# Two RMS norms applied as factors after the products, activations kept in freed buffers, and four PSUM banks per product

## The chip, the cores and the metric

The kernel runs on one core of one Trainium2 chip. The metric is device time in microseconds (us) of one execution. The engines are TensorE (PE: matmuls, with its weight loads listed apart as PEld), VectorE (DVE), ScalarE (ACT), GpSimd (POOL, which issues the gathers of table rows here) and SyncE (SP, which issues the other DMAs). Matmul results go to PSUM, of which this kernel uses all eight banks of 128 x 512 floats; all else lives in SBUF.

## The reference

One layer of a hybrid decoder is computed for 512 prompt tokens and 64 sample tokens together (576 columns), with D = 1024:

```
xn = rmsnorm(x) * attn_norm_g;  z = xn @ w_in          # q k v su sv gate_a gate_b: 30 blocks of 128 columns
a  = window attention(q, k, v);  m = gelu(su) * spatial_gate(LN(gelu(sv)))
x1 = x + (sigmoid(g_a) * (a @ w_branch_a) + sigmoid(g_b) * (m @ w_branch_b)) @ w_out
t  = rmsnorm(x1) * ffn_norm_g
s  = (t @ w_q) . sub_keys                              # 8 heads, two halves, 128 keys each
best 16 of the sums of the two halves' top 16;  gate = softmax(best)
x2 = x1 + sum_k gate_k * gelu(t . U[idx_k]) * V[idx_k] # 16384 experts
x3 = x2 + sigmoid(rmsnorm(x2) @ w_ple_gate) * (p @ w_ple)
```

A norm's factor 1/rms is one positive number per token. So it can be applied to a product's result as well as to its input, and the top 16 of a token's scores are the same with or without it; only the softmax of them needs it.

## The kernel before, in words

The work is tiled by 128. Every weight and every left operand is split in two fp32r parts, `hi` and `lo` (`split`: an ACT copy, then a DVE subtraction), and a product is three matmuls per 128 of depth (`tform`): 24 matmuls for a full product. `joint` makes a product for the 576 tokens in two halves of 256 and 320 columns, each in one PSUM bank from `mm()`, a pool of two banks, and hands each to an eviction. `load_block` loads a weight block of 512 KB (four buffers) and splits it (three buffers for each part), at high priority.

The stages, in the order in which TensorE comes to them:

1. `normed(xT, ...)`: squares of the eight pieces of x (`sumsq`, ACT), summed (DVE); ten small matmuls with ones give a column of sums, `rs` is 1/rms, a diagonal of it times ones gives the factor as a row in PSUM. Then each piece is multiplied (DVE, L164) and split: 16 pieces of half the columns.
2. The 30 blocks of `w_in` (`w_chunk`), evicted by ACT (copy, gelu or sigmoid). Attention and the spatial gate run beside them, one step after each block.
3. `w_br`: eight blocks, in each the two branches, evicted by DVE (L475).
4. `w_out`: eight blocks; x1 = result + x, again squares and sums. The per-layer embedding product `ple` fills in behind.
5. `normed(x1, ...)`, the second norm: as in 1, and it keeps copies of two groups of tokens, which `make_xr` turns by 16 transposes into rows for the gathers.
6. `peer_wq`: 16 query blocks (`joint`), each followed by the scores against 128 keys (`key_scores`), of which DVE finds the top 16 for each of five token tiles.
7. The experts. 128 prompt and 64 sample tokens use gathered rows (POOL fetches a row of U or V per token and choice; DVE multiplies and sums). The other 384 tokens go through all experts: `stage1(j)` is a product of 24 matmuls of 384 columns with the j-th block of U and a gelu; `build_g(tb)` makes the gates of 16 tokens as one-hot matrices on ACT and DVE and multiplies them on TensorE, and writes them to DRAM (`gd`); `stage2` multiplies activations by gates and adds the product with the j-th block of V to six PSUM banks.
8. The last norm and gate, and the output.

Stage 7 has an order of its own. `retrieve` (DVE, some ACT) is the choice of the 16 experts of a token tile, in steps; `stage1` calls stand between its steps. 62 calls of `stage1` come before the first `stage2`: the first NSP go out to DRAM (`ad`) and are read back later; 35 stay in a ring of RING buffers. In the last loop, over j, the first NSP + 1 turns have `stage2` alone, the next 66 have a `stage1` and a `stage2` each, and the rest `stage2` alone. `pay` sets how many gathered rows are fetched per turn.

A scheduler sets the order of the instructions on each engine from the order of the code and from priorities. Each engine takes its instructions strictly in that order, so an instruction that waits holds up all behind it on its engine.

Of the kernel before, what the change touches and what calls it, by code (L numbers as in the profile page):

```python
# [17 lines left out]
P = 128  # L18
D = 1024
# [9 lines left out]
NSP = 27  # L29
NAS = 12  # L30
# [7 lines left out]
RING = 36  # L38
# [8 lines left out]
def tile_decoder_step(ctx: ExitStack, tc: tile.TileContext, a, o):  # L47
# [74 lines left out]
    def tt():  # L122
        return e1.tile([P, NT], F32, name="t", bufs=4)
# [22 lines left out]
    def normed(x, tot, bk, gcol, hi, lo, keep=None):  # L146
        ps = bk()
        for c0, r in TILES:
            T.matmul(ps[:r, c0 // P:c0 // P + 1], lhsT=tot[:, c0:c0 + r], rhs=ones[:, 0:1], start=True, stop=True)
        rs = e1.tile([P, 5], F32, name="rs", bufs=1)  # L150
        for r, c in ((P, slice(0, 4)), (NS, slice(4, 5))):
            A.activation(rs[:r, c], ps[:r, c], AF.Sqrt, scale=1.0 / D, bias=eps[:r, 0:1])
            V.reciprocal(rs[:r, c], rs[:r, c])
        for cols in HALVES:
# [7 lines left out]
            for k in range(KC):  # L162
                xn = tt()[:, cols]
                V.scalar_tensor_tensor(xn, x[k][:, cols], vecs[:, gcol + k:gcol + k + 1], rstd,  # L164
                                       op0=ALU.mult, op1=ALU.mult)
                split(xn, hi[k][:, cols], lo[k][:, cols])
                if keep is not None:
                    keep(k, xn, cols)
# [16 lines left out]
    w_chunk(0, lambda ps, cols: A.activation(kraw[:, cols], ps, AF.Copy))  # L185
    bo = cload("blockones", [P, P])
# [259 lines left out]
    for i in range(24):  # L446
        if i < 8:
            t, g = (svT, suT)[i // 4], i % 4
            w_chunk(6 + i, lambda ps, cols: A.activation(t[:, g, cols], ps, AF.Gelu_apprx_tanh))
        else:  # L450
# [20 lines left out]
    for c in range(KC):  # L471
        w = load_block(a["w_br"][c])
        for i, (x, k0_) in enumerate(((ahl, 0), (mhl, 4))):
            sg = sgs[2 * c + i]
            joint(w, x, lambda ps, cols: V.tensor_tensor(sg[:, cols], sg[:, cols], ps, op=ALU.mult), k0_, 4)  # L475
# [40 lines left out]
    xk, xd = row((P, KC, P)), row((P, KC, 2, NS))

    def keep(k, xn_, cols):
        if cols.start == 0:
            A.activation(xk[:, k, :], xn_[:, 0:P], AF.Copy)  # L520
        else:
            A.activation(xd[:, k], xn_[:, 512 - cols.start:][:, None, :].to_broadcast([P, 2, NS]), AF.Copy)

    xn2_4 = [[x4(), x4()] for _ in range(2)]
    xn2 = [[q[k // 4][:, k % 4, :] for k in range(KC)] for q in xn2_4]
# [6 lines left out]
    tk = pool(tks, "tk", 2, "right")

    def make_xr():
        for src in (xd.rearrange("p k u t -> p k (u t)"), xk):
            xr_t = gp.tile([P, D], F32, name="xr")
            for hh in range(2):
                pt = bank("pt")
                for k in range(4):
                    T.transpose(out=pt[:, k * P:(k + 1) * P], in_=src[:, hh * 4 + k, :], identity=ident)  # L540
                A.activation(xr_t[:, hh * 512:(hh + 1) * 512], pt, AF.Copy)
            xrs.append(xr_t)
# [543 lines left out]
```

## Time and profile before

| | us |
|---|---|
| three runs | 1824.76, 1827.74, 1828.55 |
| median | 1827.74 |
| the profiled execution | 1827.41 |
| its span in the trace | 1825.7 |
| TensorE busy | 1771.8 (97%) |
| VectorE busy | 1417.3 (78%) |
| ScalarE busy | 871.0 (48%) |
| GpSimd busy | 531.6 (29%) |

The profile is of one execution. Lines such as L81 are lines of the kernel's file; nearly all products have L81, since a helper records them, so the tile names tell them apart: `x` is the split input, `c` a tile of a pool of large ones, `mm`, `sc`, `pt` and `pv` are PSUM banks, `oacc` the six accumulators of stage 2. A row of the view of waits reads "who <- whom: us in total, times, longest us". A row of a view by stretches gives, for each engine, busy us and the number of instructions, then TensorE's granted clock as a share of full speed, the share of time in which the DMA engines were busy, and GB/s.

### The profile page before, as it was taken

What the parts mean: (1) busy time and instruction counts of PE and PEld (TensorE: products, weight loads), DVE (VectorE), ACT (ScalarE), POOL (GpSimd) and SP (SyncE); (2) the same over time, 40 slices, a digit from 0 to 9 for tenths busy, and PEclk for the clock granted to TensorE, in tenths of its full rate; (3) what the DMA queues carried; (4) which work ended last, traced back from release to release, by engine and by line L of the source; (5) the groups of instructions that cost most, each with busy time, mean ns of one, the idle gap of its engine ahead of it and who ended that gap; (6) DMA issues with size and microseconds to landing.
All of it is one profiled execution on the core that took longest, in us unless ns stands there. A gap on an engine that the chain in (4) does not pass through costs nothing.

```text
span 1825.7 us, 27790 instructions
## 1 busy us (share of the span) xinstructions
PE 1771.8 (97%) x10094; PEld 1599.7 (88%) x10094; DVE 1417.3 (78%) x2846; ACT 871.0 (48%) x1560; POOL 531.6 (29%) x390
## 2 busy tenths in 40 slices
PE   6999999999998999999998999999999999999998
PEld 5987998989998999999976799989989899987776
DVE  6245446547889999999778898888888888899963
ACT  5476434244235688999732333333333333333441
POOL 0000000000002111455124565544444545466500
PEclk9999999999999999999999999999999999999999
DMA  7211223351226686999999999999999999999842
GB/s 222 86 47 47 70 79 125 115 165 64 74 72 207 217 249 221 342 355 348 336 333 346 355 410 393 356 372 331 357 378 325 361 370 327 326 348 376 325 133 75
DMA packets 177465, 458.18 MB, mean 251 GB/s; under 512 B 15664, under 2 KB 77872, under 8 KB 175280
## 3 DMA queue, kind: packets, MB, share of 16 engines
q1 hardware_dynamic: 121744, 254.34, 40.1%
q0 software_dynamic: 55584, 202.07, 30.2%
q8 instruction: 79, 1.29, 0.3%
q14 instruction: 58, 0.48, 0.1%
HBM read 419.72 MB, written 37.36 MB: 250 GB/s over the span
## 4 chain that ended last, share of the span: by engine, by line
PE 55%; DVE 3%; DMA 3%; issue 3%; POOL 1%; ACT 1%; DVEq 0%; POOLq 0%; ACTq 0%
PE mm L81 25%; PE oacc L907 23%; PE sc L792 2%; DMA x1c<-ad 2%; PE oacc L867 2%; PE pv L792 1%; PE pt L792 1%; POOL row L679 1%; DVE acc L698 1%; PE mm L867 1%; DVE w_lo L66 1%; DMA gs<-gd 1%; DMA row<-peer_v,idx 0%; DVE wl L66 0%; ACT w_hi L65 0%
## 5 line engine op out<-in xcount | busy, mean ns | idle before, releaser
L81 PE MATMUL mm<-x,w_hi 128*128 128x384 f32 (+2 forms) x3776 | 911.0, 326 | 14.7 <-ACT aS L745 8.9
L81 PEld LDWEIGHTS mm<-x,w_hi 128*128 128x128 f32 x3776 | 655.9, 191 | 36.4 <-ACT aS L745 11.1
L81 PE MATMUL mm<-x,w_lo 128*128 128x384 f32 (+2 forms) x1888 | 609.4, 323 | 0.0
L65 ACT ACTIVATE w_hi<-w_raw 128x1024 fp32r<-128x1024 f32 x325 | 344.0, 1059 | 452.7 <-PE mm L81 356.0
L66 DVE TENSOR_TENSOR w_lo<-w_raw,w_hi 128x1024 fp32r<-128x1024 f32 x325 | 396.5, 1221 | 150.8 <-ACT w_hi L65 145.9
L679 POOL DMA_INDIRECT row<-peer_u,idx x192 | 254.0, 1323 | 890.7 <-DVE pos L600 537.2
L81 PEld LDWEIGHTS mm<-x,w_lo 128*128 128x128 f32 x1888 | 359.0, 190 | 3.4 <-issue 3.2
L679 POOL DMA_INDIRECT row<-peer_v,idx x192 | 276.1, 1438 | 268.4 <-DVE acc L698 233.4
L907 PE MATMUL oacc<-w_hi,wl 128*128 128x512 f32 x768 | 244.1, 400 | 7.0 <-DVE wl L66 7.0
L907 PE MATMUL oacc<-w_hi,wh 128*128 128x512 f32 x768 | 244.9, 399 | 5.8 <-ACT wh L65 5.8
L698 DVE SCALAR_TENSOR_TENSOR acc<-row,wts,acc 128x1024 f32<-128x1024 f32 x192 | 245.2, 1277 | 2.3 <-DMA row<-peer_v,idx 2.0
L907 PE MATMUL oacc<-w_lo,wh 128*128 128x512 f32 x768 | 243.5, 398 | 0.0
L691 DVE SCALAR_TENSOR_TENSOR row<-row,xr 128x1024 f32<-128x1024 f32 x192 | 231.0, 1217 | 3.3 <-DMA row<-peer_u,idx 3.2
L907 PEld LDWEIGHTS oacc<-w_hi,wl 128*128 128x128 f32 x768 | 145.1, 190 | 44.8 <-DVE wl L66 10.4
L907 PEld LDWEIGHTS oacc<-w_lo,wh 128*128 128x128 f32 x768 | 145.7, 190 | 35.5
L907 PEld LDWEIGHTS oacc<-w_hi,wh 128*128 128x128 f32 x768 | 144.0, 189 | 37.3 <-ACT wh L65 7.7
L65 ACT ACTIVATE wh<-aL 128x384 fp32r<-128x384 f32 x65 | 34.1, 525 | 160.3 <-PE oacc L907 154.5
L781 ACT ACTIVATE oa<-oa,ew 128x128 f32<-128x128 f32 x192 | 86.0, 488 | 0.3
L780 ACT ACTIVATE oa<-c_iota,ew 128x128 f32<-128x128 f32 x192 | 67.2, 397 | 0.0
L792 PE MATMUL sc<-ob,oa 128*128 128x128 f32 x384 | 60.1, 279 | 1.4 <-DVE ob L783 1.3
L65 ACT ACTIVATE wh<-aS 128x384 fp32r<-128x384 f32 x36 | 18.9, 525 | 88.8 <-PE oacc L907 88.8
L66 DVE TENSOR_TENSOR wl<-aL,wh 128x384 fp32r<-128x384 f32 x65 | 36.6, 564 | 29.7 <-ACT wh L65 29.1
(293 smaller groups left out, 1721.3 us busy)
## 6 DMA issues: line engine op xcount, KB each, us to landing
w_raw<-peer_uT SPq DMA_DIRECT2D x128, 512.0 KB, 6.5
w_raw<-peer_v SPq DMA_DIRECT2D x128, 512.0 KB, 6.5
gd<-gs SPq DMA_DIRECT2D x24, 1024.0 KB, 9.1
gs<-gd SPq DMA_DIRECT2D x16, 1536.0 KB, 10.2
w_raw<-w_in SPq DMA_DIRECT2D x30, 512.0 KB, 3.3
w_raw<-peer_wq SPq DMA_DIRECT2D x16, 512.0 KB, 3.4
ad<-aS SPq DMA_DIRECT2D x27, 192.0 KB, 4.3
x1c<-ad SPq DMA_DIRECT2D x27, 192.0 KB, 5.5
```

The source lines that it names most:

```text
L65: A.activation(hi, src, AF.Copy)
L66: V.tensor_sub(lo, src, hi.bitcast(F32))
L81: mark_pe[0] = T.matmul(ps, lhsT=w[wi][:, wk + k, :], rhs=x[xi][k], start=i == 0, stop=i == n - 1)
L679: ins = G.indirect_dma_start(out=row_, out_offset=None, in_=table, in_offset=bass.IndirectOffsetOnAxis(ap=ix, axis=0))
L691: V.scalar_tensor_tensor(row_, row_, 1.0, xrs[ti], op0=ALU.mult, op1=ALU.mult, accum_out=dots[:, s:s + 1])
L698: V.scalar_tensor_tensor(accs[ti], row_, wts[:, s:s + 1], accs[ti], op0=ALU.mult, op1=ALU.add)
L780: A.activation(oa[:, t, :], iota, AF.Abs, bias=ew[:, 0, c + t:c + t + 1])
L781: A.activation(oa[:, t, :], oa[:, t, :], AF.Relu, scale=ew[:, 4, c + t:c + t + 1], bias=ew[:, 2, c + t:c + t + 1])
L792: T.matmul(pt[:, t * P:(t + 1) * P], lhsT=oa[:, t, :], rhs=ob[:, t, :], start=True, stop=True)
L867: T.matmul(ps[hh][:r], lhsT=xi[:, k, :r], rhs=w[k][wi][:, hh * 512:(hh + 1) * 512], start=k == 0 and xi is xh and wi == 0, stop=k == KC - ...
L907: mark_pe[0] = T.matmul(oacc[t][hh], lhsT=wi[:, ts], rhs=vi[:, hh * 512:(hh + 1) * 512], start=j == 0 and last == 0 and vi is vh, stop=j = ...
```

## The change

- The first norm: x times `attn_norm_g`, without 1/rms, is split and goes into the `w_in` products. 1/rms is copied to SBUF as a row `rn`, and every eviction of a `w_in` product becomes a DVE multiplication by `rn`; gelu, sigmoid and the query's square then run on ACT in place. The squares, their sums and `rn` have a raised priority. The first weight block is loaded between the second and third piece of x.
- The second norm: x1 times `ffn_norm_g` is split in the `w_out` loop (`xg`) and goes into the 16 query products. The factor enters the softmax as the scale of its exponential. The rows for the gathers come straight from the transposes of x1 (eight more small matmuls double the sample tokens), multiplied by factor and gain (DVE). The normed input of `stage1` is made later, in query blocks 3 to 10 (`norm_x`), from x1 in DRAM.
- `w_br`: the second branch's halves go to the two `sc` banks. `stage1`: every other product goes to the two `pv` banks until the last loop, and `build_g` uses `sc` and `pt` alone.
- Buffers: 24 of the ring's activations and six for those on their way to DRAM lie in tiles of the pool `x4`, which is free by then. RING goes from 36 to 44 and NSP from 27 to 19, so still 62 calls of `stage1` come first.

```diff
-NSP = 27
-NAS = 12
+NSP = 19
-RING = 36
+RING = 44
+NXP = 24
...
-def joint(w, x, out, wk=0, nk=KC):
+def joint(w, x, out, wk=0, nk=KC, bk=mm):
...
-    add(k, xT[k])
-normed(xT, tot, lambda: bank("sc"), 0, *xn)
+    with tc.high_priority(offset=500):
+        add(k, xT[k])
+    A.activation(xn[0][k], xT[k], AF.Copy, scale=vecs[:, k:k + 1])
+    V.scalar_tensor_tensor(xn[1][k], xT[k], vecs[:, k:k + 1], xn[0][k].bitcast(F32),
+                           op0=ALU.mult, op1=ALU.subtract)
+rn = e1.tile([P, NT], F32, name="rn", bufs=1)
+with tc.high_priority(offset=500):
+    for cols, ps in rstd_rows(tot, lambda: bank("sc")):
+        A.activation(rn[:, cols], ps, AF.Copy)
...
-def w_chunk(c, out):
-    joint(load_block(a["w_in"][c]), xn, out)
+def w_chunk(c, dst, out):
+    def scaled(ps, cols):
+        with tc.high_priority(offset=1000):
+            V.tensor_tensor(dst[:, cols], ps, rn[:, cols], op=ALU.mult)
+        out(cols)
+    joint(load_block(a["w_in"][c]) if c else first, xn, scaled)
...
     joint(w, x, lambda ps, cols: V.tensor_tensor(sg[:, cols], sg[:, cols], ps, op=ALU.mult), k0_, 4,
+          (mm, lambda: bank("sc"))[i])
...
+    A.activation(xg[0][c], x1[c], AF.Copy, scale=gcol)
+    V.scalar_tensor_tensor(xg[1][c], x1[c], gcol, xg[0][c].bitcast(F32), op0=ALU.mult, op1=ALU.subtract)
...
-normed(x1, tot, lambda: bank("sc"), 8, *xn2, keep=keep)
+rstd_cols(tot, rs2)
+def norm_x(k):
+    xc = tq.tile([P, NB], F32, name="xc")
+    S.dma_start(xc, x1d[k])
+    V.scalar_tensor_tensor(xc, xc, vecs[:, 8 + k:9 + k], rn2, op0=ALU.mult, op1=ALU.mult)
+    split(xc, xn2[0][:, k, :], xn2[1][:, k, :])
...
-A.activation(gt, gt, AF.Exp)
+A.activation(gt, gt, AF.Exp, scale=rs2[:, b_:b_ + 1])
...
-ps = mm()[:, :NB]
+ps = (mm() if j % 2 or phase[0] > 1 else bank("pv"))[:, :NB]
```

Three places show how the order of instructions moves. The first is DVE at the start of the program. Before (`rstd` is the sum of squares, `x` the split input):

```order
L141 TENSOR_TENSOR rstd<-rstd,t 128x576 x7
L153 RECIPROCAL rs<-rs 128x4
L153 RECIPROCAL rs<-rs 64x1
L66 TENSOR_TENSOR w_lo<-w_raw,w_hi 128x1024
L164 SCALAR_TENSOR_TENSOR t<-c_90,c_vecs,sc 128x256 x3
L66 TENSOR_TENSOR x_106<-t,x_104 128x256 x3
```

After, with the first evictions of `w_in` products (L191) at its end:

```order
L181 SCALAR_TENSOR_TENSOR x_112<-c_92,c_vecs,x_110 128x576
L141 TENSOR_TENSOR rstd<-rstd,t 128x576
L181 SCALAR_TENSOR_TENSOR x_113<-c_93,c_vecs,x_111 128x576 x2
L153 RECIPROCAL rs<-rs 128x5
L181 SCALAR_TENSOR_TENSOR x_113<-c_93,c_vecs,x_111 128x576 x2
L207 CAST cst<-c_tabs 128x48
L66 TENSOR_TENSOR w_lo<-w_raw,w_hi 128x1024
L191 TENSOR_TENSOR t<-mm,rn 128x256
```

The low parts of x no longer stand behind `rs`; the last two of them still do, and the first eviction stands behind all of it.

The second is DVE in the attention, at a softmax of one block (`sm` is its sum, which ACT makes). Before:

```order
L266 TENSOR_SCALAR nm<-mx 128x4
L272 TENSOR_TENSOR sm<-sm,es 128x4
L273 RECIPROCAL sm<-sm 128x4
L275 TENSOR_SCALAR s<-s,sm 128x128 x4
L288 SCALAR_TENSOR_TENSOR s<-sc,rq,b_656 128x128 x4
```

After:

```order
L277 TENSOR_SCALAR nm<-mx 128x4
L191 TENSOR_TENSOR c_628<-mm,rn 128x256
L283 TENSOR_TENSOR sm<-sm,es 128x4
L284 RECIPROCAL sm<-sm 128x4
L286 TENSOR_SCALAR s<-s,sm 128x128 x4
L191 TENSOR_TENSOR c_628<-mm,rn 128x320
```

Evictions now stand on DVE's queue between the steps of the softmax, the second of them behind a step that waits for ACT.

The third is TensorE at the end of the one-hot products (L792 before, L819 after; `xd` is the input of `stage1`), where `stage2` begins. Before, the last of them is followed by 74 matmuls of `stage1`, which begin so:

```order
L792 MATMUL pv<-ob,oa 128x128
L81 MATMUL mm<-x_3910,w_hi 128x384
L81 MATMUL mm<-x_3908,w_lo 128x384
L81 MATMUL mm<-x_3907,w_hi 128x384
L81 MATMUL mm<-x_3909,w_hi 128x384
```

After, by 13:

```order
L819 MATMUL sc<-ob,oa 128x128
L81 MATMUL mm<-xd,w_lo 128x384
L81 MATMUL mm<-xd,w_hi 128x384 x2
L81 MATMUL mm<-xd,w_lo 128x384
L81 MATMUL mm<-xd,w_hi 128x384 x2
L81 MATMUL mm<-xd,w_lo 128x384
L81 MATMUL mm<-xd,w_hi 128x384 x2
L81 MATMUL mm<-xd,w_lo 128x384
L81 MATMUL mm<-xd,w_hi 128x384 x2
L81 MATMUL mm<-xd,w_lo 128x384
L931 MATMUL oacc<-w_hi,wh 128x512 x2
```

So 61 matmuls have moved from behind the one-hot products to ahead of or between them. At the other end of that stretch, 20 products of `stage1` stand ahead of the first step of `build_g`, where 17 stood.

More of the change, by code (lines that the diff above doesn't have):

```diff
@@ L144, in sumsq, with rstd_cols, rstd_rows @@
         return tot, add
-    def normed(x, tot, bk, gcol, hi, lo, keep=None):
-        ps = bk()
+    def rstd_cols(tot, rs):
+        ps = bank("sc")
         for c0, r in TILES:
-            T.matmul(ps[:r, c0 // P:c0 // P + 1], lhsT=tot[:, c0:c0 + r], rhs=ones[:, 0:1], start=True, stop=True)
+            for p0 in range(0, P, r):
+                T.matmul(ps[p0:p0 + r, c0 // P:c0 // P + 1], lhsT=tot[:, c0:c0 + r], rhs=ones[:, 0:1],
+                         start=True, stop=True)
+        A.activation(rs, ps[:, 0:5], AF.Sqrt, scale=1.0 / D, bias=eps[:, 0:1])
+        V.reciprocal(rs, rs)
+    def rstd_rows(tot, bk):
         rs = e1.tile([P, 5], F32, name="rs", bufs=1)
-        for r, c in ((P, slice(0, 4)), (NS, slice(4, 5))):
-            A.activation(rs[:r, c], ps[:r, c], AF.Sqrt, scale=1.0 / D, bias=eps[:r, 0:1])
-            V.reciprocal(rs[:r, c], rs[:r, c])
+        rstd_cols(tot, rs)
         for cols in HALVES:
@@ L161, in normed @@
                          start=True, stop=True)
[L162 to L168, printed above, removed]
+            yield cols, rstd
+    vecs = cload("vecs", [P, 18])
     xT = f8(f4)
@@ L172, in tile_decoder_step @@
         S.dma_start(xT[k], a["xT"][k])
-    vecs = cload("vecs", [P, 18])
+        if k == 1:
+            first = load_block(a["w_in"][0])
     ident = cload("ident", [P, P])
@@ L510, in tile_decoder_step @@
         for hh in range(2):
+            hs = slice(hh * 512, (hh + 1) * 512)
             pt = bank("pt")
             for k in range(4):
-                T.transpose(out=pt[:r, k * P:(k + 1) * P], in_=x1[hh * 4 + k][:, c0:c0 + r], identity=ident)
-            A.activation(acc_t[:r, hh * 512:(hh + 1) * 512], pt[:r], AF.Copy)
-        accs.append(acc_t)
[L516 to L525, printed above, removed]
-    normed(x1, tot, lambda: bank("sc"), 8, *xn2, keep=keep)
+                x1k = x1[hh * 4 + k][:, c0:c0 + r]
+                T.transpose(out=pt[:r, k * P:(k + 1) * P], in_=x1k, identity=ident)
+                if r == NS:
+                    T.matmul(pt[NS:, k * P:(k + 1) * P], lhsT=x1k, rhs=ident, start=True, stop=True)
+            A.activation(acc_t[:r, hs], pt[:r], AF.Copy)
+            V.scalar_tensor_tensor(xr_t[:, hs], pt, rs2[:, c0 // P:c0 // P + 1], grow[:, hs],
+                                   op0=ALU.mult, op1=ALU.mult)
+        accs.append(acc_t)
+        xrs.append(xr_t)
     e1s.close()
     c4s.close()
+    xds = ExitStack()
+    xdp = pool(xds, "xd", 2, "right")
+    xn2 = [xdp.tile([P, KC, NB], F32R, name="xd") for _ in range(2)]
     tqs = ExitStack()
@@ L531, in tile_decoder_step, with norm_row @@
     tks = ExitStack()
[L532 to L542, printed above, removed]
+    tk = pool(tks, "tk", 1, "right")
+    rn2 = tq.tile([P, NB], F32, name="rn2", bufs=1)
+    def norm_row():
+        ps = bank("pt")[:, :NB]
+        for b in range(3):
+            dg = tq.tile([P, P], F32, name="dg")
+            A.activation(dg, ident, AF.Copy, scale=rs2[:, b + 1:b + 2])
+            T.matmul(ps[:, b * P:(b + 1) * P], lhsT=ones, rhs=dg, start=True, stop=True)
+        A.activation(rn2, ps, AF.Copy)
+    def norm_x(k):
[3 more added lines that the diff above has]
+        split(xc, xn2[0][:, k, :], xn2[1][:, k, :])
     TOPK = ((4, 4), (0, 8), (1, 8), (2, 8), (3, 8))
@@ L728, in tile_decoder_step @@
     acp = []
-    xb = [[t[:, P:512] for t in xi] for xi in xn2]
-    ds = ExitStack()
+    xb = [[x[:, k, :] for k in range(KC)] for x in xn2]
+    ds, aLs, sps = ExitStack(), ExitStack(), ExitStack()
     def stage1():
@@ L762, in tile_decoder_step @@
     tqs.close()
-    aSs = ExitStack()
-    aS = pool(aSs, "aS", NAS)
+    held_x = [xp.tile([P, 6, NB], F32, name="x4") for _ in range(NXP // 6)]
     gs_s = ExitStack()
-    ep = pool(gs_s, "ep", 3)
+    ep = pool(gs_s, "ep", 2)
     gsp = pool(gs_s, "gsp", 2)
@@ L829, in tile_decoder_step @@
         stage1()
+    phase[0] = 2
     gs_s.close()
@@ L877, in tail_out @@
             S.dma_start(o["y"][c0:c0 + r, hs], sg[:r, hs])
-    def spare(shape=(P, D), dt=F32):
-        return xp.tile(list(shape), dt, name="x4")
     def gathered(ti):
```

93 lines of the change are left out of this document (53 added, 40 removed).

## The prediction

> **What bounds the kernel now.** The engine totals and the stretches come first. In a row of stretches stand the busy time of PE, PEld, DVE, ACT and POOL with instruction counts, then TensorE's granted clock.
>
> ```profile
> PE 1771.8 (97%) x10094; PEld 1599.7 (88%) x10094; DVE 1417.3 (78%) x2846; ACT 871.0 (48%) x1560; POOL 531.6 (29%) x390
> ...
> 285.40:342.70 57.30, 54.70 (x382) 51.78 (x381) 33.34 (x55) 17.15 (x22) 0.00 (x0) 1.00 0.35 118
> ...
> 394.02:428.24 34.22, 31.23 (x183) 27.01 (x182) 20.32 (x42) 25.53 (x64) 0.00 (x0) 0.90 0.30 103
> 428.24:539.60 111.36, 111.36 (x824) 106.98 (x823) 93.74 (x523) 33.83 (x66) 0.00 (x0) 1.00 0.23 75
> ...
> 539.60:900.66 361.06, 348.16 (x2193) 337.38 (x2193) 351.63 (x981) 298.98 (x643) 110.25 (x76) 0.99 0.84 280
> ...
> 900.66:915.48 14.82, 13.05 (x74) 12.74 (x74) 5.07 (x6) 6.70 (x11) 0.00 (x0) 1.00 0.85 293
> 915.48:1050.80 135.32, 125.67 (x505) 97.98 (x506) 110.36 (x131) 41.77 (x56) 58.90 (x39) 0.95 0.95 344
> ...
> 1055.70:1608.90 553.20, 553.20 (x2774) 500.00 (x2773) 481.27 (x628) 193.12 (x262) 279.55 (x214) 1.00 0.96 358
> 1609.00:1684.00 75.00, 75.00 (x323) 60.40 (x323) 71.80 (x72) 27.28 (x36) 49.56 (x35) 1.00 0.98 366
> ```
>
> They are, in order: eight pairs of `w_br`; the second norm, from the last `w_out` matmul to the third query product; the other query blocks; the one-hot products; the matmuls behind the last of these; the 28 turns of `stage2` alone; the turns with both stages; late turns of `stage2` alone. TensorE sets the pace nearly everywhere, and since the change removes little of its work, only its waits and half-clock time can be won. One stretch is different: over 361.06 us DVE is busy 351.63 and TensorE 348.16, so there DVE leads. PE's waits name the same places:
>
> ```profile
> PE sc L149 <- DVE rstd L141: 12.4, 1, 12.4
> PE mm L81 <- ACT aS L745: 8.9, 3, 3.7
> PE oacc L907 <- DVE wl L66: 7.0, 6, 1.8
> PE oacc L907 <- ACT wh L65: 5.8, 4, 2.5
> PE sc L160 <- ACT pw L159: 3.5, 3, 2.0
> ...
> PE mm L81 <- DVE c L475: 2.6, 7, 0.7
> ```
>
> The sum is made against the profiled execution, 1827.4 us, which stands 0.3 below the median.
>
> **First norm.** First the timeline (start, us, engine, operation), then `L81` alone to 33.24, and all engines from 25.55.
>
> ```profile
> 7.44 3.74 ACT L139 ACTIVATE t<-c 128x576 f32<-128x576 f32 x5 [0.42 <-DMA c<-xT]
> 8.15 4.21 DVE L141 TENSOR_TENSOR rstd<-rstd,t 128x576 f32<-128x576 f32 x5 [0.35 <-ACT t L139]
> 11.20 1.28 ACT L143 ACT_TABLE_LOAD   x1
> ...
> 15.44 1.04 ACT L65 ACTIVATE w_hi<-w_raw 128x1024 fp32r<-128x1024 f32 x1
> ...
> 16.51 1.23 DVE L66 TENSOR_TENSOR w_lo<-w_raw,w_hi 128x1024 fp32r<-128x1024 f32 x1 [1.30 <-ACT w_hi L65]
> ...
> 19.02 0.88 PE L81 MATMUL mm<-x,w_hi 128*128 128x256 f32 x2
> ...
> 25.55 0.57 PE L81 MATMUL mm<-x,w_hi 128*128 128x256 f32 x1 [2.16 <-DVE x L66]
> ...
> 0.00:33.24 33.24, 11.88 (x49) 10.57 (x49) 0.90 0.73 247
> ...
> 25.55:33.24 7.69, 7.51 (x30) 6.78 (x30) 7.38 (x20) 4.09 (x9) 0.86 (x2) 0.56 0.96 359
> ```
>
> The first product starts at 19.02 and has its 48 matmuls behind it at 33.24, ragged, with 0.44 x 7.69 = 3.4 us lost to the clock. Afterwards the matmuls follow the pieces of x. The earliest second product is fixed by three chains. ACT: the squares end at 7.44 + 3.74 = 11.2; the weight block loaded in their midst is 0.52 MB, at the 247 GB/s that end the row of the first 33.24 us 2.1 us, so 13.3. Then come the table (1.28), four high parts (priced as squares, 3.74/5 = 0.75 each, 3.0), the root, four diagonals (0.4 each, an estimate from their place in the timeline between 15.44 and 19.02), and one weight part (1.04): about 21. DVE: eight low parts and seven sums at 4.21/5 = 0.84, 12.6, with two `w_lo`, mostly paced by ACT: about 20 to 22. Last, both banks of `mm` are taken by the first product, and they come free by an eviction that needs `rn`: about 22.5, plus 0.5 each. So the second product starts near 24.3, and 33.24 - 24.3 = 8.9 is gained. Of that I give 2.4 back, since the second product may now be the one at half clock: -6.5. Bounds: -10 (no loss, and 1 us earlier) to -3 (the load of x is 2 us later still, the clock loss is whole).
>
> **w_br.** Four banks in place of two take away the seven waits on L475, 2.6 us in all. Each pair of branches had two banks for four halves, so nothing is late next but the weights; -2.6, between 0 (they wait for `w_lo` instead) and -4.2 (the gaps under the view's resolution too, some 0.2 us in each of eight blocks).
>
> **Second norm.** Rows of stretch and timeline, and DVE's largest groups of norm and query blocks (busy, mean ns, idle before).
>
> ```profile
> 405.09 1.43 PE L160 MATMUL sc<-pw,ones 128*128 128x128 f32 x8 [2.05 <-ACT pw L159]
> ...
> 408.00:420.00 12.00, 11.42 (x57) 9.64 (x56) 10.86 (x27) 8.81 (x30) 0.00 (x0) 0.72 0.09 29
> ...
> L164 DVE SCALAR_TENSOR_TENSOR t<-c,c_vecs,sc 128x320 f32<-128x320 f32 x8 | 4.0, 541 | 0.0
> ...
> L66 DVE TENSOR_TENSOR w_lo<-w_raw,w_hi 128x1024 fp32r<-128x1024 f32 x15 | 18.4, 1225 | 22.6 <-ACT w_hi L65 22.6
> ```
>
> PE idles 34.22 - 31.23 = 2.99, and the half clock behind its 2.05 us wait costs 0.28 x 12.00 = 3.36. With `xg` split during `w_out`, the first query product needs no factor, and both go: -6.3. PE's own work: 16 transposes go and 8 small matmuls for the doubled sample rows come in; the passes for the factor's row shrink from 10 to 6 and move to query block 1 (1.43/8 = 0.18 each). That is within 1 us of nothing. Bounds: -3 (a wait stays for the last high part, and the clock drops again) to -8.
>
> `norm_x` adds to query blocks 3 to 10 one load of 0.2 MB on SP each, a multiplication of 384 columns (541 ns for 320, so 0.65) and a low part (0.45 to 0.65): eight times 1.1 to 1.3, about 9.5 us of DVE. DVE has 111.36 - 93.74 = 17.6 idle there, so it fits: 0, at worst +3 if top-16 steps fall behind. Queued behind it on DVE is `w_lo`, which the next product waits for.
>
> **w_in evictions.** ACT's 60 evictions become DVE's, at
>
> ```profile
> L475 DVE TENSOR_TENSOR c<-c,mm 128x320 f32<-128x320 f32 x16 | 7.7, 483 | 12.3 <-PE mm L81 12.3
> L475 DVE TENSOR_TENSOR c<-c,mm 128x256 f32<-128x256 f32 x15 | 6.2, 416 | 9.2 <-PE mm L81 9.2
> ...
> 387.61 0.40 PE L81 MATMUL mm<-c,w_hi 128*128 128x256 f32 x2
> ...
> 390.49 0.46 PE L81 MATMUL mm<-c,w_hi 128*128 128x320 f32 x2
> ```
>
> 30 x (0.483 + 0.416) = 27 us more on DVE, ACT keeping its function on SBUF. A bank must be free before the next half is done, and a half of 256 columns takes 390.49 - 387.61 = 2.88 us. An unlucky eviction stands behind a `w_lo` (1.225) and two steps of the attention, for which I take the size of L164 above (0.54 each): 1.225 + 1.08 + 0.48 = 2.8, just under 2.88, so a late one now and then. In the mean there is room, and the evictions are ordered first: 0, with a rival for the contrary.
>
> **One-hot stretch.** Where it ends:
>
> ```profile
> 900.27 0.38 PE L792 MATMUL pv<-ob,oa 128*128 128x128 f32 x2
> ...
> 901.31 0.38 SPq L794 DMA_DIRECT2D gd<-gs  x1
> ...
> 906.83 0.33 SPq L926 DMA_DIRECT2D gs<-gd  x1
> ...
> 914.09 1.07 DVE L933 TENSOR_TENSOR x1c<-x1c,gs 128x384 f32<-128x384 f32 x2 [2.43 <-DMA x1c<-ad]
> ...
> 915.48 0.73 PE L907 MATMUL oacc<-w_hi,wh 128*128 128x512 f32 x2 [1.77 <-ACT wh L65]
> ```
>
> From the last one-hot matmul the gates go out and return through DRAM, 5.5 us from issue to issue and 7.3 more to the product with them. Before, 74 matmuls (13.05 us) lie under these 14.8 us. Now 13 do, 13/74 x 13.05 = 2.3, so about 12.5 us are bare. But the 61 moved ones (10.8 us) go into a stretch where PE idles 361.06 - 348.16 = 12.9 and DVE leads: they should fit into PE's idle time, and the round trip ends as long after the last one-hot matmul as before. What moves with them is two more `w_lo` ahead of the last one-hot matmul, 2 x 1.225 = +2.4, and the clock drops behind the bare wait: 3.4 x half, +1.7, since the first turns wait for gates anyway. Against that, more products lie ahead of the first `build_g`, which can fill a part of DVE's 361.06 - 351.63 = 9.4 idle: -1.6. Sum +2.5. Bounds: -7 (the 9.4 go whole, the `w_lo` stay) and +12.5 (no moved matmul finds idle time, 10.8, and the clock 1.7). Fewer banks for `build_g` (four for six) delay only its copies.
>
> **Turns of stage2 alone.** 135.32/28 = 4.83 us each; the late ones take 75.00/(323/18) = 4.18. The waits on `wl` and `wh` (7.0 + 5.8) lie here, behind read-backs of gates and spilled activations. Eight turns move to the both-stage loop, which shows PE busy throughout. By proportion 8 x 0.65 = -5.2; but the first turns' waits stay, so -3.5 (bounds -1, -5.2). The spills' 8 stores and 8 loads on SP go with them. The loop itself and the end, 0: DVE's 71.80 of 75.00 is near its limit, and nothing is added there.
>
> Sum: -6.5 - 2.6 - 6.3 + 2.5 - 3.5 = -16.4; 1811.0 for the profile, 1811 for the median.
>
> [...]
>
> **Rivals.** (1) The stretch wins: DVE's idle time vanishes. For it: DVE leads there. Against: its idle time is spread over many waits. -9.4 in place of +2.5: 1799. (2) The stretch loses: the round trip is bare, and the moved matmuls find no hole since waits on `aS` (8.9) lie elsewhere: +12.5 in place of +2.5, 1821. (3) The first norm changes nothing: `rn` comes as late as `x` did, and two banks still hold the second product: 1811 + 6.5 = 1818. For it: the eviction stands behind everything on DVE. (4) Slower: the 60 evictions make TensorE wait, each behind a softmax step that itself waits for ACT. DVE's 33.34 of 57.30 us in `w_br` speaks against a full engine, the 2.8 against 2.88 above for late ones. It decides from (1827.7 + 3.7 - 1811)/60 = 0.34 us for each; at 0.6, 36 us, 1847.
>
> **How the numbers follow.** The sum 0.50 (its own range 1804 to 1816), (1) 0.17, (2) 0.15, (3) 0.08, (4) 0.10. A range of 1798 to 1822 leaves out (4) and some of the edges of (1) and (2). Within 0.2% of 1827.7, 3.7 us, is about what a measurement cannot tell from no change: from the cases, faster 0.84 (all of the first two, most of (2) and (3)), same 0.08, slower 0.08.
>
> **What the profile after would show.** First product near 10 us, second near 24; no wait on L475's successor; query products right behind `w_out` at full clock; the bare wait of about 12 us ahead of the first `oacc`, with PE's idle time before it gone; 20 turns of 4.9 us. Wrong would be: PE waits on the evictions in the attention, a one-hot stretch that grows by the moved matmuls, or clock drops of 3.4 us at new waits.

## The result, and the profile after

| | before | after |
|---|---|---|
| median, us | 1827.37 | 1796.99 |
| runs, us | 1824.76 to 1828.55 (4) | 1793.91 to 1799.59 (4) |
| the profiled execution, us | 1827.41 | 1799.59 |
| its span, us | 1825.7 | 1797.8 |

The ratio is 0.9831, 95% interval 0.9813 to 0.9849: 30.9 us faster (27.6 to 34.2). The forecast was 16.4 us and its range ended at 1798, so the direction was right and the size was not.

The engine totals of the changed kernel, and its stretches in the order of the prediction's: `w_br`; second norm, from the last `w_out` matmul to the first scores; the other query blocks; one-hot products; the stretch behind them; 20 turns of `stage2` alone; both stages; late turns.

```profile
PE 1748.1 (97%) x10094; PEld 1576.2 (88%) x10094; DVE 1434.5 (80%) x2876; ACT 866.7 (48%) x1523; POOL 542.0 (30%) x390
...
271.40:325.80 54.40, 54.36 (x392) 52.95 (x391) 34.82 (x59) 17.68 (x24) 0.00 (x0) 1.00 0.40 132
...
376.71:402.41 25.70, 25.70 (x172) 22.05 (x170) 10.14 (x13) 13.46 (x24) 0.00 (x0) 1.00 0.46 152
403.44:512.95 109.51, 109.51 (x827) 105.13 (x826) 100.75 (x537) 37.46 (x75) 0.00 (x0) 1.00 0.27 88
512.95:877.62 364.67, 356.29 (x2254) 343.13 (x2254) 356.36 (x986) 301.81 (x645) 109.22 (x76) 0.99 0.83 276
877.62:895.15 17.53, 2.53 (x17) 2.21 (x15) 3.47 (x5) 3.19 (x7) 0.94 (x1) 0.72 0.92 318
895.15:992.87 97.72, 90.32 (x360) 70.34 (x361) 78.05 (x94) 29.81 (x40) 42.12 (x27) 0.95 0.88 327
997.00:1545.70 548.70, 548.70 (x2777) 496.04 (x2777) 482.73 (x636) 193.00 (x261) 289.00 (x214) 1.00 0.97 362
1556.00:1656.00 100.00, 100.00 (x431) 80.56 (x430) 96.99 (x97) 36.41 (x48) 66.57 (x48) 1.00 0.99 371
```

TensorE has no idle time in the second norm (25.70 of 25.70 us) and a granted clock of 1.00; it does 2.53 us of work in 17.53 behind the last one-hot matmul. Its waits:

```profile
PE oacc L931 <- ACT wh L65: 18.0, 3, 15.0
PE mm L81 <- ACT x L180: 10.1, 2, 9.9
PE oacc L931 <- DVE wl L66: 6.4, 6, 2.0
PE pt L783 <- DVE e L657: 3.2, 1, 3.2
PE mm L81 <- DVE w_lo L66: 1.8, 2, 1.0
```

No wait on an eviction is left, of `w_in` or of `w_br`. The start, in the timeline:

```profile
9.90 1.44 PE L81 MATMUL mm<-x,w_hi 128*128 128x256 f32 x3 [9.90 <-ACT x L180]
...
11.14 0.42 PE L81 MATMUL mm<-x,w_lo 128*128 128x256 f32 x1
...
14.74 1.28 ACT L143 ACT_TABLE_LOAD   x1
...
16.14 2.76 ACT L180 ACTIVATE x<-c,c_vecs 128x576 fp32r<-128x576 f32 x4
...
19.60 0.28 PE L81 MATMUL mm<-x,w_lo 128*128 128x256 f32 x1
...
20.09 1.49 ACT L163 ACTIVATE pw<-c_ident,rs 128x128 f32<-128x128 f32 x4 [0.26 <-DVE rs L153]
...
21.49 1.04 ACT L65 ACTIVATE w_hi<-w_raw 128x1024 fp32r<-128x1024 f32 x1
...
23.70 0.42 DVE L191 TENSOR_TENSOR t<-mm,rn 128x256 f32<-128x256 f32 x1
...
24.18 0.51 PE L81 MATMUL mm<-x,w_hi 128*128 128x256 f32 x2
```

The chain on ACT is the one that the prediction added up, and the second product starts at 24.18, right behind the first eviction. A 256-column matmul takes 0.42 us at 11.14 and 0.28 at 19.60: the slow matmuls of the start lie under the arrival of x, and the second product has none (0.28 us again at 24.52).

Every stage can be measured between matmuls that both kernels have. The lengths are differences of start times in the trace, us; the two columns on the right are experiments that are told below.

| from the matmul before, to | before | after | before, weights 32 bytes on | after, weights placed first |
|---|---|---|---|---|
| first `pv<-t,c_blockones` (start) | 39.77 | 30.63 | 40.39 | 31.39 |
| last `sc<-wmS` (w_in) | 219.05 | 216.37 | 217.54 | 218.09 |
| first of `w_out` (end of w_in, w_br) | 83.91 | 78.96 | 83.41 | 79.43 |
| last of `w_out` | 51.12 | 50.75 | 50.74 | 51.08 |
| first scores (second norm) | 33.03 | 25.70 | 32.95 | 27.31 |
| last scores (query blocks) | 112.45 | 110.54 | 110.31 | 112.68 |
| last one-hot matmul | 361.03 | 364.67 | 362.82 | 367.32 |
| first `oacc` | 15.11 | 17.53 | 14.87 | 17.46 |
| first of `add_x1` (28 or 20 turns) | 135.29 | 97.72 | 140.58 | 93.58 |
| last of `stage1` (both stages) | 557.88 | 552.77 | 552.77 | 558.44 |
| last of `stage2` | 152.36 | 187.05 | 152.38 | 186.79 |

Each column is one execution. In kernels told of below that leave a stage as it is and have the same spacing of matmuls, one trace differs from another by up to 2 us in `w_in` and 3 us in the turns of `stage2` alone, by about 1 us in the start, the one-hot stretch, the wait behind it and the last row, and by less than 0.1 us in `w_br`, `w_out`, the second norm, the query blocks and the turns with both stages.

Three rows were not in the prediction: `w_in` and the query blocks are shorter, and so are the turns with both stages, by 5.1 us, although TensorE was busy all the time, or nearly so, in these before (218.86 of 219.05, 111.36 of 111.36 and 553.20 of 553.20 us) and their products are as many. For the last two that is far more than the scatter.

### The profile page after: what moved, and what is told of

It reads as the page before. It is cut to its first block, busy times and chain, and to the rows that moved or that the text cites. A ratio compares the mean times of both kernels' runs of the same rounds, so it can differ in the third digit from the quotient of the medians.

```text
span 1797.8 us, 27777 instructions
## 1 busy us (share of the span) xinstructions
PE 1748.1 (97%) x10094; PEld 1576.2 (88%) x10094; DVE 1434.5 (80%) x2876; ACT 866.7 (48%) x1523; POOL 542.0 (30%) x390
## 4 chain that ended last, share of the span: by engine, by line
PE 86%; DVE 5%; DMA 4%; issue 3%; ACT 1%; POOL 0%; SPq 0%; DVEq 0%; ACTq 0%; POOLq 0%
PE mm L81 41%; PE oacc L931 25%; PE pv L81 6%; PE sc L819 2%; DMA x1c<-ad 2%; PE pt L819 2%; PE oacc L894 2%; PE sc L81 1%; DVE w_lo L66 1%; PE sc L579 1%; PE pv L446 1%; PE pv L314 1%; PE sc L296 1%; DVE acc L725 1%; PE mm L894 1%
## 5 line engine op out<-in xcount | busy, mean ns | idle before, releaser
L81 PE MATMUL mm<-xd,w_hi 128*128 128x384 f32 x1552 | 405.6, 340 | 0.5 <-ACT w_hi L65 0.5
L81 PE MATMUL mm<-x,w_hi 128*128 128x256 f32 (+1 forms) x1600 | 328.9, 299 | 10.4 <-ACT x L180 10.1
L81 PEld LDWEIGHTS mm<-xd,w_hi 128*128 128x128 f32 x1552 | 281.1, 189 | 6.0 <-ACT w_hi L65 0.8
L81 PEld LDWEIGHTS mm<-x,w_hi 128*128 128x128 f32 x1600 | 256.8, 189 | 24.4 <-ACT x L180 10.5
L81 PE MATMUL mm<-xd,w_lo 128*128 128x384 f32 x776 | 263.8, 340 | 1.8 <-DVE w_lo L66 1.8
L81 PE MATMUL mm<-x,w_lo 128*128 128x256 f32 (+1 forms) x800 | 235.8, 295 | 0.0
L81 PEld LDWEIGHTS mm<-x,w_lo 128*128 128x128 f32 x800 | 151.1, 189 | 1.1 <-issue 0.8
L81 PEld LDWEIGHTS mm<-xd,w_lo 128*128 128x128 f32 x776 | 146.7, 189 | 2.5 <-DVE w_lo L66 2.5
L81 PE MATMUL pv<-xd,w_hi 128*128 128x384 f32 x496 | 136.5, 347 | 0.7 <-ACT x L774 0.7
L65 ACT ACTIVATE wh<-x 128x384 fp32r<-128x384 f32 x69 | 36.3, 526 | 168.4 <-PE oacc L931 162.5
```

What stands on the lines that cost most here:

```text
L65: A.activation(hi, src, AF.Copy)
L81: mark_pe[0] = T.matmul(ps, lhsT=w[wi][:, wk + k, :], rhs=x[xi][k], start=i == 0, stop=i == n - 1)
```

## The experiments

### Where the weights lie

In the turns with both stages TensorE is never idle in either kernel (553.20 of 553.20 us before, 548.70 of 548.70 after), so its matmuls must follow each other more closely. Read from start to start of neighbours in one bank, the mean spacing at 384 columns was 176.6 ns before and 173.4 after, at 256 columns 119.7 and 116.1 (a few tenths of a ns hang on which pairs are counted); at 320 and 512 columns it was the same within 0.3 ns. What did change is the place of the weight blocks: three tiles left the pool of constants that lies ahead of them and one came in, 1248 bytes less in all. The split inputs kept their place from the other end of SBUF, at the same address modulo 256. In the first experiment the kernel before got one unused tile of 32 bytes:

```diff
+    V.memset(const.tile([P, 8], F32, name="pad"), 0.0)
     wp = pool(ctx, "wp", 2)
```

> The kernel before with one unused tile of 32 bytes more in the pool of constants, so that every weight block and all else on that side of SBUF lies 32 bytes further on (weights at 32 modulo 64 instead of 0; the split inputs x stay at 32). Theory 1 (addresses: the products' matmuls of 256 and 384 columns are spaced closer after the change, 173.5 ns on the mean instead of 176.6 at 384 columns, because the change moved the weights by 1248 bytes, which is 32 modulo 64): the spacing goes from 176.6 to 173.5 here too, and the time falls by what w_in (4.6), the query blocks (1.9), the turns with both stages (5.3) and w_out (0.4) gained that no step of the prediction had, some 12 us, to 1815. Rival (the spacing comes from something that the change does, its banks, its fewer buffers or its scheduling): spacing stays 176.6, 1827.

Measured: 1820.95, ratio to before 0.9949 (0.9931 to 0.9968), 9.3 us faster. The spacing was 173.4 and 116.3, the changed kernel's. (The profiled execution is the slowest of the four, 1825.47: in the table above it gains 1.5 us in `w_in`, 2.1 in the query blocks and 5.1 in the turns with both stages, but its 28 turns of `stage2` alone took 5.3 us more.) The stretch from 1120 to 1520 us lies in the turns with both stages in all kernels; the second number in it is the count of matmuls. In the kernel before:

```profile
1120.00:1520.00 400.00, 400.00 (x1990) 360.84 (x1989) 342.92 (x469) 140.57 (x192) 195.23 (x157) 1.00 0.96 355
```

The kernel before with 32 bytes more:

```profile
1120.00:1520.00 400.00, 400.00 (x2010) 361.12 (x2009) 344.82 (x474) 142.71 (x193) 204.64 (x159) 1.00 0.97 357
```

The changed kernel:

```profile
1120.00:1520.00 400.00, 400.00 (x2011) 361.20 (x2010) 345.35 (x462) 142.06 (x193) 205.42 (x159) 1.00 0.96 353
```

Twenty more matmuls in the same 400 us, with the same clock and no idle time in either. The same padding in the changed kernel:

> The changed kernel with the same 32 bytes added to the constants: weights back at 0 modulo 64, x at 32. Theory 1: spacing at 384 columns goes back to 176.6, time rises by some 12 us to 1809. Rival: 1797 and 173.5.

Measured: 1797.10, ratio to before 0.9824 (0.9805 to 0.9844), no loss; spacing 173.6 and 117.0. The weights lie at 0 modulo 64 here, as in the kernel before, which had 176.6 and 119.7: their address modulo 64 alone does not give the spacing. The next shifts the other side, with a pool of 32 bytes placed ahead of the pool of x:

> The changed kernel with 32 bytes added at the start of the other side of SBUF instead: x at 0 modulo 64, weights at 32 as in the changed kernel. If what counts is that x and weights lie in the same half of 64 bytes: slow spacing, 1809. If the weights' address alone counts: 1797. Rival (no addresses): 1797.

Measured: 1797.95, ratio 0.9826 (0.9809 to 0.9842); spacing 173.65 and 117.0, and its most frequent values are those of the run before (175, 172, 171 ns at 384 columns; 116 and 117 at 256). These two have the same distance from weights to x, while both addresses differ. Both paddings together:

> The changed kernel with both paddings: x at 0, weights at 0 modulo 64. If the same half counts: 1797. If the weights' address alone counts: 1809. Rival (no addresses): 1797.

Measured: 1803.24, ratio 0.9862 (0.9844 to 0.9879); 174.1 and 119.5. Neither shift alone cost time, and both together did, which fits the distance between the two and neither address by itself. Modulo what? 96 bytes of padding make the distance 96 modulo 128, as before, and 224 modulo 256, not as before:

> The changed kernel with an unused tile of 96 bytes in the constants, so that the distance from the weights to the split inputs is 96 modulo 128 as in the kernel before (it is 64 in the changed one). Theory 1 (the spacing of the matmuls goes by the distance of the two operands' addresses modulo 128): the mean spacing at 384 columns goes from 173.4 to 176.6 ns and at 256 columns from 116.1 to 119.7, and the time rises by what the other way gave in the kernel before, some 9 us, to 1806. Rival 1 (the change's own structure makes the spacing, and the first padding worked on the kernel before by chance): 1797, 173.5. Rival 2 (weights at 0 modulo 128 are what is slow; with 96 bytes more they stand at 0 too, so this run can't tell that from theory 1).

Measured: 1803.15, ratio 0.9867 (0.9851 to 0.9884); 174.2 and 118.4. Slower, but not with the 176.6 and 119.7 of before: these two distances are equal modulo 128 and their spacings are not. The last of this line puts the distance at 96 modulo 256 without any padding:

```diff
-    const = pool(ctx, "const", 1)
     wp = pool(ctx, "wp", 2)
+    const = pool(ctx, "const", 1)
```

> The changed kernel with the pool of weights placed ahead of the pool of constants: nothing else moves, and the distance from the weights to the split inputs is 96 modulo 256 as in the kernel before (64 in the changed one). So far, by that distance modulo 256, mean spacing at 256 and 384 columns was: 96 (before) 119.7 and 176.6; 64 (changed, and before with 32 bytes) 116.1 to 116.3 and 173.4; 32 (two kernels) 117.0 and 173.6; 0 119.5 and 174.1; 224 (the run with 96 bytes) 118.4 and 174.2. Theory (the distance modulo 256 sets the spacing): 119.7 and 176.6, and the time rises by some 9 us to 1806. Rival 1 (modulo 128, which the run with 96 bytes speaks against): 118.4 and 174.2, 1803. Rival 2 (the change's structure): 116.1 and 173.4, 1797.

Measured: 1809.69, ratio to before 0.9897 (0.9876 to 0.9919); spacing 176.6 and 119.7, the numbers of before in the changed kernel. Its row of the same stretch:

```profile
1120.00:1520.00 400.00, 400.00 (x1990) 361.00 (x1990) 341.63 (x462) 140.74 (x191) 197.77 (x156) 1.00 0.96 350
```

| distance x - weights, modulo 256 | kernels | spacing at 256 columns, ns | at 384, ns |
|---|---|---|---|
| 96 | before; after with weights first | 119.65; 119.71 | 176.61; 176.58 |
| 64 | after; before + 32 | 116.09; 116.29 | 173.42; 173.42 |
| 32 | after + 32; after, x shifted | 116.98; 117.00 | 173.60; 173.65 |
| 0 | after, both | 119.54 | 174.14 |
| 224 | after + 96 | 118.35 | 174.17 |
| 128 | four products held, + 192 (below) | 118.51 | 175.79 |

That the spacing went with the distance in these nine kernels is shown by moving one side, the other and both, and by the two pairs at 96 and 64, whose distances from the weights to the x of `w_in` differ by 3584 and 1280 bytes and whose spacings agree within 0.2 ns. A padding moves all that lies behind it on its side of SBUF; only the kernel with the weights first moves the weights against everything else but the constants. That the table goes by the distance modulo 256 is an estimate of the author's from these two pairs (3584 and 1280 are multiples of 256) and from 96 and 224, which are equal modulo 128 and whose spacings differ by 1.3 and 2.4 ns; no run tried a third such pair. Why the spacing went with the distance was not shown, and the distance is not all: at 64, the mean at 256 columns is made of some 117 ns in `w_in` and 114 in the query blocks, alike in the two kernels.

At 512 columns nearly all matmuls are those of `stage2`, and both of their operands lie on the side of the weights. The paddings leave their distance as it is, so they say nothing of 512 columns. Only the kernel with the weights first changes it, and there the spacing is 234.0 ns in place of 233.2.

### The parts, one by one

The first norm ahead of the products again (each piece times gain and 1/rms, then split), with the evictions left on DVE as copies:

```diff
...
-            A.activation(rn[:, cols], ps, AF.Copy)
+            for k in range(KC):
+                xk = tt()[:, cols]
+                V.scalar_tensor_tensor(xk, xT[k][:, cols], vecs[:, k:k + 1], ps, op0=ALU.mult, op1=ALU.mult)
+                split(xk, xn[0][k][:, cols], xn[1][k][:, cols])
...
-                V.tensor_tensor(dst[:, cols], ps, rn[:, cols], op=ALU.mult)
+                V.tensor_copy(dst[:, cols], ps)
```

> The changed kernel with its first norm before the products again: each piece of x times gain and 1/rms, then split; the evictions stay DVE's, as copies. Theory (prediction's first step): w_in starts some 9 us later, 1806, with the same time from the first attention matmul to the spatial gate's last as in the changed kernel (216 to 218 us). Rival (the late start is made up later in w_in, or the evictions' factor costs time): 1797 to 1800, or a shorter w_in.

Measured: 1807.63, ratio to before 0.9890 (0.9871 to 0.9909), some 10.8 us above the changed kernel by the two ratios. The first products start at 19.77 again:

```profile
PE sc L150 <- DVE rstd L141: 14.0, 1, 14.0
...
19.77 0.86 PE L81 MATMUL mm<-x,w_hi 128*128 128x256 f32 x2
```

The start took 40.46 us to the first `pv<-t,c_blockones` in place of 30.63, and `w_in` 216.40 in place of 216.37. The first norm is worth 9.8 us; within the 2 us by which `w_in` scatters, nothing of it is lost later, and the factor at the evictions costs nothing.

`w_br` with both branches in the two `mm` banks:

```diff
-     joint(w, x, lambda ps, cols: V.tensor_tensor(sg[:, cols], sg[:, cols], ps, op=ALU.mult), k0_, 4,
-          (mm, lambda: bank("sc"))[i])
+     joint(w, x, lambda ps, cols: V.tensor_tensor(sg[:, cols], sg[:, cols], ps, op=ALU.mult), k0_, 4)
```

> The changed kernel with both branches of w_br in the two mm banks, as before. Theory (prediction's step): seven waits on the eviction come back, +2.6 to +4.5 us, 1800 to 1801. Rival (the stage gained by the matmuls' spacing alone): 1797, no waits.

Measured: 1801.88, ratio 0.9870 (0.9846 to 0.9893). The seven waits are back:

```profile
PE mm L81 <- DVE c L487: 2.8, 7, 0.8
```

The stage took 83.53 us in place of 78.96: 4.6 us for 2.8 of idle time in the view of waits. The row counts from the modelled end of a matmul to the next start. From start to start, six of the seven waits have 0.64 us in place of some 0.15, and the spacing after each is 0.1 us longer too: 0.6 us for each, where the row counts 0.34.

Spilled activations and ring as before (28 turns ahead of the loop with both stages):

```diff
-NSP = 19
+NSP = 27
-RING = 44
+RING = 36
```

> The changed kernel with 27 spilled activations and a ring of 36, as before, so 28 turns of stage2 alone instead of 20. Theory (prediction's step): eight turns move from the end, where they take 4.18 us, to the front, where they take 4.83 to 4.89: +5, at least the 2.9 that the two traces showed, so 1800 to 1802. Rival (the front's loss is a fixed price of the first turns): 1797.

Measured: 1802.51, ratio 0.9864 (0.9847 to 0.9880), against 0.9831 of the changed kernel some 6 us more, with intervals that just meet. Its 28 turns took 133.46 and its end 152.72, together 286.2 where the changed kernel has 284.8. That is 1.4 us, less than these turns scatter; 2.0 more stand in `w_in`, which the edit does not touch. The sign is that of the step, and its size is open, somewhere between 1 and 6.

### The bare wait behind the one-hot products

After the change the round trip of the gates is bare:

```profile
878.55 0.38 SPq L821 DMA_DIRECT2D gd<-gs  x1
...
883.80 0.33 SPq L953 DMA_DIRECT2D gs<-gd  x1
884.18 0.90 SPq L958 DMA_DIRECT2D x1c<-ad  x2
...
893.98 1.03 DVE L960 TENSOR_TENSOR x1c<-x1c,gs 128x384 f32<-128x384 f32 x2 [10.46 <-DMA x1c<-ad]
...
895.15 1.22 PE L931 MATMUL oacc<-w_hi,wh 128*128 128x512 f32 x2 [15.00 <-ACT wh L65]
```

It is the largest wait of TensorE in the program, and looks like the next thing to win. Two kernels cover it. One puts all of `stage1` into the two `mm` banks, as before:

```diff
-        ps = (mm() if j % 2 or phase[0] > 1 else bank("pv"))[:, :NB]
+        ps = mm()[:, :NB]
```

> The changed kernel with all products of stage1 in the two banks of mm, as before the change. In the order of instructions 74 matmuls then stand behind the last one-hot matmul again, where the changed kernel has 13. Theory 2 (as in the prediction: DVE leads in the one-hot stretch, the moved matmuls lay in TensorE's idle time there, and only the w_lo that moved with them cost anything): the wait of 15.0 us at the first oacc goes, but the stretch is hardly shorter; 1793 to 1796, or 1797 where TensorE waits for banks again. Rival (the moved matmuls lengthen the stretch, because DVE's and TensorE's waits there alternate): 10 us less, 1787.

Measured: 1798.94, ratio 0.9846 (0.9828 to 0.9863), not faster than the changed kernel. The wait of 15 us is gone, and waits on activations are back; below them the one-hot stretch and the one behind it:

```profile
PE mm L81 <- ACT x L774: 11.7, 4, 4.4
...
512.57:880.95 368.38, 350.63 (x2193) 337.31 (x2193) 353.56 (x983) 299.76 (x640) 108.31 (x76) 0.98 0.81 270
880.95:895.81 14.86, 13.10 (x77) 12.78 (x75) 5.16 (x6) 6.70 (x11) 0.00 (x0) 1.00 0.86 290
```

The other keeps the four banks and holds four products behind the last one-hot matmul by an order alone:

```diff
-S1_END = 6
+S1_END = 4
...
+                if i == 0 and hold[0] is not None:
+                    after(mark_pe[0], hold[0])
...
+                last_oh[0] = T.matmul(pt[:, t * P:(t + 1) * P], lhsT=oa[:, t, :], rhs=ob[:, t, :], start=True,
+                                      stop=True)
...
+    hold[0] = last_oh[0]
     while nlive < RING - 1:
         stage1()
+    hold[0] = None
```

> The changed kernel with its four last products of stage1 ahead of stage2 held behind the last one-hot matmul (an order alone, four banks kept): 93 matmuls, 16.1 us, lie under the round trip of the gates instead of 13. Theory 2: the bare wait goes from 15.0 to 1 or 2 us, the one-hot stretch loses only four w_lo of 1.22 us on DVE, so some 4 us in all, 1793. Rival (TensorE's queue sets the pace there): the stretch loses the 80 moved matmuls, 13.8 us, 1783.

Measured: 1795.64, ratio 0.9823 (0.9807 to 0.9840). The two stretches:

```profile
514.02:877.99 363.97, 347.16 (x2173) 333.30 (x2173) 352.88 (x983) 298.92 (x640) 109.73 (x76) 0.98 0.82 274
877.99:894.23 16.24, 16.24 (x97) 16.24 (x96) 5.08 (x6) 5.64 (x9) 0.00 (x0) 1.00 0.77 255
```

All 16.24 us behind the one-hot products are now work, 80 matmuls more of it, and yet the stretch ahead lost only 0.7 us: TensorE idles 16.8 us there in place of 8.4. DVE is busy 352.88 of 363.97. Together the two stretches are 2.0 us shorter, which the times cannot tell from nothing. So the wait of 15 us was not worth its length: filled with work from the stretch ahead, it came back there as idle time. That DVE sets the pace of that stretch is the reading of its busy time; no run made DVE's work there shorter.

The same kernel with 192 bytes more in the constants tried one more distance:

> The kernel with four products held behind the last one-hot matmul, with 192 bytes more in the constants: distance 128 modulo 256, not seen so far. Theory of the distance: a spacing of its own, somewhere between 116 and 120 at 256 columns and 173 and 177 at 384, and the time follows it by some 2.5 us for each ns at 256 and 384 columns; 1793 to 1804. Rival (no distances): 116.1 and 173.4, 1795.

Measured: 1799.10, ratio 0.9858 (0.9829 to 0.9886); 118.5 and 175.8 ns. By the medians that is 3.5 us slower than without the padding, as its spacing says, but the intervals overlap. No kernel tried is clearly faster than the changed one.

## Why the prediction was wrong in its size

At the same distance from weights to x, the changed kernel is 18.8 us faster than before (0.9897, 14.8 to 22.7), where the sum said 16.4. Taking the 9.3 us of the 32 bytes off the whole gives 21.6; the kernel with the weights first has also lost some 2 us in the 2304 matmuls of `stage2`, at 234.0 in place of 233.2 ns. Term by term, in us of the two traces, which differ by 27.8 (the spacing by the ratio of the padded kernel):

| step | predicted | measured | by |
|---|---|---|---|
| first norm | -6.5 | -9.1 | start; +9.8 when undone |
| `w_br` | -2.6 | -4.6 | undone |
| second norm | -6.3 | -7.3 | first scores |
| `w_in` evictions, `norm_x` | 0 | 0 | see below |
| one-hot stretch and round trip | +2.5 | +6.1 | 376.1 to 382.2 |
| turns of `stage2` alone | -3.5 | -2.9 | 287.7 to 284.8, within the scatter |
| spacing of the matmuls | none | -9.3 | kernel before + 32 bytes |

The step that failed stands ahead of the sum: "since the change removes little of its work, only its waits and half-clock time can be won". TensorE was busy for 400.00 of 400.00 us at a clock of 1.00 in both kernels, and yet did 1990 matmuls in one and 2011 in the other; some 3 ns on each of 30 x 24 matmuls of `w_in`, 16 x 24 of the queries and 66 x 24 of the turns with both stages were to be won, in the last alone 5.1 us, and "The loop itself and the end, 0" missed it. Nothing in the one trace of before could show a second spacing; that three tiles were moved out from ahead of the weights was in the diff.

The steps that the sum did have come to -17.8, close to its -16.4: it held for what the change does, and lacked what the change did by the way. That it held so closely is in part luck: three of them were too small by 5.6 us together, and two too favourable by 4.2.

The first norm: the second product came at 24.18 where 24.3 was worked out. The 2.4 us given back for the half clock (0.50 from 25.60 to 32.42 us in the trace of before) were wrong, because the slow matmuls now lie where x has yet to arrive (0.41 us for 256 columns at 16.66). `w_br`: the step was right and its size was that of the idle row, not of the gap; the bound of -4.2 was the better reading. The second norm: both the idle time and the half clock (0.50 from 407.89 to 414.72 us before) went, as said, and PE stands at 25.70 of 25.70 us at a clock of 1.00.

The evictions (rival 4) cost nothing:

```profile
L191 DVE TENSOR_TENSOR c<-mm,rn 128x320 f32<-128x320 f32 x24 | 11.8, 491 | 54.7 <-PE mm L81 54.7
L191 DVE TENSOR_TENSOR c<-mm,rn 128x256 f32<-128x256 f32 x24 | 10.2, 423 | 22.5 <-PE mm L81 22.4
```

They take the 483 and 416 ns of the rows they were priced from, within 8 ns, and DVE waits for TensorE ahead of them, not the other way round. `norm_x` brought DVE from 93.74 of 111.36 to 100.75 of 109.51 us in the query blocks; the kernel before with 32 bytes more needs 110.31 from first to last scores, the changed one 110.54.

The one-hot stretch was right in kind: the trip is bare (15.0 us forecast as some 12.5), the moved matmuls took TensorE's idle time (12.9 down to 8.4), DVE leads. The size was off by 3.6 us, in three places. The stretch itself grew by 3.6 us where 2.4 was said, since three more low parts of weights stand on DVE there, not two; first before, then after:

```profile
L66 DVE TENSOR_TENSOR w_lo<-w_raw,w_hi 128x1024 fp32r<-128x1024 f32 x58 | 70.8, 1221 | 3.5 <-ACT w_hi L65 2.9
...
L66 DVE TENSOR_TENSOR w_lo<-w_raw,w_hi 128x1024 fp32r<-128x1024 f32 x61 | 74.4, 1219 | 0.2
```

They make 3.6 of the 4.7 us by which DVE's work grew. The 1.6 of idle time that was to be won back came to 1.1, and the rest of DVE's growth took it. And the trip did not end "as long after the last one-hot matmul as before" but 2.4 us later. The read-back of the first spilled activation was issued as soon as before, and the multiplication that waits for it began 9.8 us after the issue (884.18 to 893.98), before 6.9:

```profile
907.21 0.90 SPq L931 DMA_DIRECT2D x1c<-ad  x2
...
914.09 1.07 DVE L933 TENSOR_TENSOR x1c<-x1c,gs 128x384 f32<-128x384 f32 x2 [2.43 <-DMA x1c<-ad]
```

Why that load took longer is open; in two of the padded kernels it was 8.4 and 8.6 us, and the trip 15.5 and 15.7. The third place is the clock behind the bare wait, forecast as +1.7, an estimate: half of a loss of 3.4 us, which is what 6.8 us at 0.50 had cost behind the waits of 2.16 and 2.05 us before. No run shows the +1.7 as an addition. The granted clock was 0.50 from 885.27 to 898.93 us, but in the kernel before it was 0.50 at the same place too, from 916.48 to 919.89, behind a wait of 1.77 us. First after, then before:

```profile
895.15:898.00 2.85, 2.85 (x7) 2.27 (x8) 1.01 (x2) 0.42 (x1) 0.00 (x0) 0.50 0.78 272
898.00:901.00 3.00, 3.00 (x13) 2.40 (x12) 1.08 (x2) 0.07 (x1) 0.00 (x0) 0.85 0.19 69
...
915.48:918.00 2.52, 2.52 (x8) 1.85 (x9) 2.52 (x4) 0.36 (x1) 0.00 (x0) 0.70 1.07 447
918.00:921.00 3.00, 3.00 (x11) 2.37 (x10) 0.43 (x1) 0.00 (x0) 0.94 (x1) 0.69 0.94 375
```

That is 1.9 us lost after (half of 2.85 and 0.15 of 3.00) and 1.7 before, so the bare wait of 15.0 us was followed by 0.2 us more of lost clock than the one of 1.77 us. Both stand in the turns of `stage2` alone, so none of it is in the 6.1.

Of the rivals, (1) came near the measured time with 1799, for another reason: DVE's idle time in the stretch did not vanish, 9.4 became 8.3. Of (2) the bare trip came true but not its price, and (3) fell with the 9.8 us of the first norm.

## What to carry to other kernels

When a kernel is bound by TensorE with no idle time left, compare the count of matmuls in equal full stretches of both traces before explaining a difference by the change: a tile of 32 bytes in another pool was worth half a per cent here. Keep the addresses of weights and inputs in mind when buffers are moved (173.4 to 176.6 ns for the same matmuls here), and test a change with one kernel in which they stand as they did. And a long wait of TensorE need not be worth its length: covering 15 us of it brought at most some 2, in a stretch where DVE is busy for 97% of the time.

## What the runs showed of the hardware

Read from start to start in the traces of nine kernels, the spacing of matmuls of 256 and 384 fp32r columns went with the distance of the two operands' SBUF addresses: 116.1 to 119.7 ns and 173.4 to 176.6 ns. Two kernels with distances 3584 bytes apart had the same spacing within 0.1 ns, and two with 1280 bytes between theirs within 0.2 ns. At 320 columns, with the same distances, it stayed at 146.6 to 146.9 ns. At 512 columns it was 233.0 to 233.4 ns in the eight kernels that keep the distance of these operands, and 234.0 in the one that changes it. The granted clock was 1.00 in the stretch from 1120 to 1520 us of the four kernels whose rows stand above, with 1990 to 2011 matmuls in it, so it does not show this.

At the start, matmuls of 256 columns took 0.42 us at 11.14 and 0.28 us at 19.60, while the row of the clock reads 1.00 from 8 us on in the changed kernel:

```profile
8.00:12.00 4.00, 1.93 (x5) 1.29 (x6) 3.00 (x5) 3.50 (x6) 0.00 (x0) 1.00 0.87 302
```

The durations show the slow start, the clock row does not. The trace has no entry of the granted clock ahead of 18.29 us (22.18 in the kernel before), and the view takes the clock as full until the first one. Ahead of these two times the matmuls are still slow, and behind them fast: 0.47 us for 320 columns at 17.87 and 0.31 at 19.96 in the changed kernel, 0.42 us for 256 columns at 21.87 and 0.28 at 22.38 in the kernel before.
